# Nine modulation steps of layer two move from layer one's attention to the end of its routing

## The chip, the cores and the metric

The kernel runs on one core of a Trainium2 chip. The metric is the device time of one execution in microseconds. Each core has five engines that work in parallel, each with its own instruction queue: PE (matrix products; a weight load stands ahead of each product), DVE and ACT (element work), POOL (element work, and the DMAs with row numbers) and SP (here only DMAs). Transfers are carried out by 16 DMA engines that all queues share.

## The reference

Two layers of a transformer block over two streams of 256 tokens with 1024 channels: x (the image) and ctx (the context). Each layer starts from a modulation vector that depends on the conditioning alone. It then runs three kinds of attention, an output projection and a mixture of 16 experts, two of which each token uses.

```python
for l in range(DEPTH):
    mod = jnp.split(silu_c @ w_ada[l] + b_ada[l], 6, axis=-1)
    sh1, sc1, g1, sh2, sc2, g2 = [m[:, None, :] for m in mod]
    ...
    hx = rms_norm(x, norm1_g[l]) * (1 + sc1) + sh1
    hc = rms_norm(ctx, norm1_g[l]) * (1 + csc1) + csh1
    mix_x, mix_c = token_mixers(hx, hc, w_in[l], ...)
    x = x + g1 * (mix_x @ w_out[l])
    hx = rms_norm(x, norm2_g[l]) * (1 + sc2) + sh2
    x = x + g2 * moe_ffn(hx, w_router, router_bias, w_gate[l], w_up[l], w_down[l])
    ...
return rms_norm(x, final_g)
```

`moe_ffn` scores a token against the router, picks two experts and sums their gated outputs. In layer one ctx goes the same way as x; in layer two ctx serves only as keys and values.

## The kernel before, in words

**Tiles and stages.** Tokens stand in tiles of 128: tiles 0 and 1 are ctx, 2 and 3 are x. Layer one computes all four, layer two only 2 and 3. A layer has four stages: the projections of the modulated tokens (w_in), the attention, the output's projection (w_out) with the routing, and the experts. Weights are float32. Most are split into two float32r parts, `whi` by ACT and `wlo` by DVE, and a product is then three matmuls (lines 197 to 199, tiles `mm`).

**The modulation.** `ada_third` (line 426) computes 2048 columns of a layer's modulation, a third. Each of its first eight steps takes one unit of w_ada (128x2048, 1 MB) and makes four products 32x512 (tile `ada`, line 448). Then come DVE's addition of the bias (`modrow`, line 454) and four transposes with small copies. A third has 9, 10 or 9 steps. They are pulled by `fill(n)` from wherever the code calls it, in a fixed order: thirds 1 and 2 of layer one, then thirds 0, 1 and 2 of layer two. `FILL` says how many steps run among a layer's projections, in its attention and in its output's projection. Third 0 (sh1 and sc1) is needed at a layer's start; thirds 1 and 2 (g1, sh2, a2, g2) from the output's projection on.

**The attention.** `attention` runs a pipeline over items: 32 in layer one, 16 in layer two. Each tick carries steps of several items and ends with up to a few `fill` steps; the steps are spread evenly over the ticks from the first item's on. The last steps of an item come up to a few ticks after its values.

**Output's projection and routing.** `out_proj` goes over the two halves of w_out's columns (`cb`) and, in each, over the tiles. After each piece it calls `Route.logits`: a square sum on ACT, four transposes, a copy (`xT`) on ACT, and the router's four products (`rps`). After a tile's second half `Route.choose` normalizes the tile, writes it to DRAM (`h2row`, 0.5 MB, on SP's queue, line 1697) and picks the experts. After the last tile this is one long chain of small DVE steps, at whose end are the positions (`pps`) and the token numbers in each expert's list (`ips`, `idx`).

**Experts.** `experts` (layer one) gathers each expert's tokens from `h2row` by number with POOL's indirect DMA (`gather`, line 1005, tile `xg`), transposes them and runs gate, up and down. `LEAD` = 4 halves of weights are split ahead. `warm(20)` makes 20 products that nothing uses, ahead of the first gather. Layer two runs experts in pairs instead (`expert_pairs`).

**The weights' order.** `Ring` holds all raw weights in the order of use, which `queue` writes. It loads the next unit as soon as a slot is free for it, all on SP's queue, where the writes of `h2row` stand too. Slots of 1 MB: four "A" slots throughout, four more in layer one from the output's projection on ("B"), two more from the experts on ("C"). Each slot has a last layer, and a unit of layer two may only take slots that live in layer two, in layer one's stages that is the four A slots. A unit that finds no slot holds those behind it:

```python
slot = next((s for s in self.free if s[2] >= self.todo[0][0][1]), None)
if slot is None:
    break
```

A slot becomes free when the engine that reads it is done, and the load on SP waits for that. The order of instructions on each engine is set by the scheduler from the order of the code, except in stretches under `manual_schedule`, where the code's own order stands (the last tile's `choose` and the attention among them).

Of the kernel before, what the change touches and what calls it, by code (L numbers as in the profile page):

```python
# [20 lines left out]
PSUM = bass.MemoryType.PSUM  # L21
# [6 lines left out]
NONE = 1024  # L28
# [4 lines left out]
# columns of the packed constants  # L33
# [3 lines left out]
# slots for raw weights: throughout, from the output projection on, from the experts on  # L37
RAW = dict(A=4, B=(4, 3), C=(2, 5))
# halves of units as float32r parts: projections, their outputs' projections, experts
WSP = dict(proj=4, out=(4, 4), moe=5)  # L40
# banks of PSUM in the phases of a layer
# [3 lines left out]
PS_MOE = dict(gu=2, y=2, tp=2, hT=1)  # L45
PS_PAIR = dict(acc=4, gu=1, w=3)
# blocks of w_in's columns: kA, qA, kB vB kC vC, qB qC and vA
CBS = (4, 2, 1, 0, 3)
# steps of modulation (whole thirds) among a layer's projections, in its attention, in its output's projection
FILL = ((0, 28, 0), (9, 10, 0))  # L50
# tiles of projections that pass before one's transposes
LATE = 2
# heads of A and pairs of heads of B and C in the attention of two tiles of queries
ORDER = "aabababaabaabbbb"
# when the last steps of heads come: ticks after the values, and where in the tick (after the evacuation, after
# the maxima, at the end)
FINISH = dict(copy=(1, 1), squares=(2, 0), scale=(3, 2), turn=(4, 2), out=(1, 2))
# steps of a tick of attention, and the item of each, counted from the tick's
TICK = (("sums", 1), ("high", 5), ("transposes", 0), ("evacuate", 0), ("weights", 1), ("finish", 0), ("scores", 3),
        ("low", 5), ("maxima", 3), ("finish", 2), ("finish", 1), ("exps", 3), ("rest", -1), ("values", -1))  # L60
# halves of experts' weights that are ready ahead of their products
LEAD = 4
OVERFLOW = True
# products that keep the array's clock up before the experts
WARM = 20
# [6 lines left out]
def shape_constants():  # L72
    """Constants that depend on shapes alone, packed [128, C_END]."""
# [25 lines left out]
class Ring:  # L99
    """Weights in the order of their use, loaded ahead into whatever slots are free."""  # L100
# [11 lines left out]
    def open(self, pool, tag, n, last, queue=None):  # L112
        """n slots, for units of layers up to last"""
        self.free.extend((pool, f"{tag}{i}" if n > 1 else tag, last) for i in range(n))
        self.load(queue)
# [42 lines left out]
    def until(self, l, queue=None):  # L158
        """Only units that layers up to l use"""
        self.upto = l  # L160
        self.load(queue)
# [6 lines left out]
class Model:  # L168
# [18 lines left out]
    def transpose4(self, in_, n=4):  # L187
        """n 128 x 128 blocks of in_, transposed, in a bank"""
# [5 lines left out]
    def mm3(self, out, xh, xl, wh, wl, start, stop):  # L194
        """out += x^T w, each operand a sum of two float32r parts"""
# [11 lines left out]
    def rstd(self, pool, ss, n, width, tag):  # L207
        """(ss / n + eps) ** -0.5 over [128, width]"""
# [12 lines left out]
    def split(self, raw, lo, hi, engine=None):  # L221
        """A half of a unit of raw weights as an exact sum of two float32r parts."""
# [7 lines left out]
    def bcast(self, pool, tag, src, n, name, bufs=1, queue=None):  # L230
        """n elements in DRAM over all partitions"""
# [46 lines left out]
    def queue(self):  # L278
        """The weights in the order of their use."""
# [15 lines left out]
        def block(name, l, cb, n):  # L295
            for h in range(2):
# [3 lines left out]
                if name == "w_out" and h:  # L300
                    # rows of heads (kind, key head, query) to chunks of (kind, query)
# [6 lines left out]
        for l in range(2):  # L308
# [4 lines left out]
            for cb in range(2):  # L313
                block("w_out", l, cb, (0, 0))
                ada(sum(spread(FILL[l][2], 8)[4 * cb:4 * cb + 4]))
# [3 lines left out]
            for ps in range(self.npass[l]):  # L319
                for e in range(NEXP):  # L320
                    for n in ("w_gate", "w_up"):
                        ring.add((n, l, ps, e), a[n][l, e].rearrange("(p k) n -> p k n", k=NKC))
                    # an expert's second part comes after the next one's first
# [13 lines left out]
    def warm(self, n):  # L337
        """Products that nothing uses: the array's clock is to be up when the next ones come"""
# [5 lines left out]
    def paired(self, l):  # L344
        """Whether the experts of a layer go two at a time, with half a list each"""
        return l == 1 and self.npass[l] == 1
# [38 lines left out]
    def columns(self, tp):  # L385
        """From transposed rows of the modulation: stream, row of 512, chunk"""
        return tp.rearrange("p (c j q) -> p q j c", j=4, q=32)[:, 0:2]

    def ada_first(self, h):
        """Half the columns of the first layer's first shift and scale: those of even chunks of d land on partitions  # L390
        0 and 32 (c), 1 and 33 (c_ctx), those of odd chunks 64 partitions on"""
# [34 lines left out]
    def ada_third(self, l, third):  # L426
        """2048 columns of the modulation: the four 512s land on partitions 32j (c) and 32j+1 (c_ctx)."""
# [42 lines left out]
        elif third == 1:  # L470
            # what the shift adds to the router's logits, over all partitions
# [25 lines left out]
    # steps and the loads of units in a third of the modulation  # L497
    STEPS = (9, 10, 9)

    def fill(self, n):  # L500
        """n steps of the modulation among other work"""
# [3 lines left out]
    # rows of the modulation in DRAM: (third, half)  # L505
# [83 lines left out]
    def parameters(self, l):  # L589
        """The small parameters of a layer's attention"""  # L590
# [19 lines left out]
        def lam():  # L610
            """-(exp1 - exp2 + lam0)"""
# [6 lines left out]
    def tokens_in(self, l, tl):  # L618
        """Steps that bring tiles of a stream, normalized and modulated, to d on the partitions in Xh and Xl"""
# [22 lines left out]
        # the chunks of d in a bank  # L642
# [35 lines left out]
    def chunk(self, ps, tiles, kc, parts):  # L678
        """The products of tiles with a chunk of d of the first block of the projections"""
# [7 lines left out]
    def first_in(self):  # L687
        """The tokens of the first layer, half of d after the other, with the first block of its projections"""
# [51 lines left out]
    def next_in(self, l):  # L740
        """The tokens of a later layer, tile by tile, with the first block of its projections"""
        ps = {}
        with self.tc.tile_pool(name="cb", bufs=1, side="right", reuse_waits="tile") as cb, self.tc.manual_schedule():
# [44 lines left out]
            # the context's tokens have had their last use  # L788
# [3 lines left out]
    def parts(self, name, l, cb, fill=(0, 0)):  # L792
        """The halves of two units, split"""
# [9 lines left out]
    def units(self, name, l, cb, pairs, xh, xl, c0, parts):  # L803
        """The products of tiles of tokens with 512 columns of a weight, a group of tiles after another."""
# [1108 lines left out]
```

## Time and profile before

| | us |
| --- | --- |
| median of 3 runs | 902.95 (902.58 to 903.57) |
| span of the profiled execution | 900.9 |
| PE busy | 799.3 (89%) |
| DVE busy | 584.3 (65%) |
| ACT busy | 453.6 (50%) |
| POOL busy | 211.5 (23%) |

The span is that of one execution recorded by the profiler; the runs' times include a little around it, 2.05 us at the median. In a row of the time line the columns are start, duration, engine, line, operation, tile written and tiles read, shapes, count, and in brackets the idle time ahead of it with what ended it. Of layer one, the attention lies in about 140 to 264 us, the output's projection in 264 to 329, the last routing steps in 329 to 346 and the experts in 347 to 505.

### The profile page before, as it was taken

To read this page: it belongs to the slowest core of one execution; us is meant where nothing else is said; L and a number is where in the kernel's file an instruction comes from. 1 tells how busy PE (TensorE), PEld (TensorE's weight loads), DVE (VectorE), ACT (ScalarE), POOL (GpSimd) and SP (SyncE) were. 2 spreads that over 40 slices of the span, in tenths; PEclk is the share of its full clock that TensorE was granted. 3 is DMA by queue.
4 is the path that set the end of the run, shared out by engine and by line. 5 is a ranking of instruction groups with operands and counts; after the bars stand their busy time and mean duration, and the time that the engine had idled before them with its cause. 6 is when DMAs were issued, how large, how long until landed. Compare 5 with 4: busy or idle time off the path is not lost.

```text
span 900.9 us, 13085 instructions
## 1 busy us (share of the span) xinstructions
PE 799.3 (89%) x4807; PEld 584.2 (65%) x4807; DVE 584.3 (65%) x1192; ACT 453.6 (50%) x877; POOL 211.5 (23%) x244
## 2 busy tenths in 40 slices
PE   4899999989889977999999459999799869999992
PEld 1578877545546746999999348767566647666551
DVE  1577673897942698899999487677587563231224
ACT  2454432777652426888888456443387442121112
POOL 2010102473320133443432561000442000000100
PEclk9999999999998998999999769999999988999996
DMA  9952221666579537899993754287035965999921
GB/s 320 346 171 92 93 94 47 249 227 235 181 239 343 192 141 261 310 402 399 402 406 146 256 202 187 90 327 281 0 132 152 354 245 220 406 406 407 378 84 51
DMA packets 52537, 213.34 MB, mean 237 GB/s; under 512 B 9756, under 2 KB 9756, under 8 KB 34672
## 3 DMA queue, kind: packets, MB, share of 16 engines
q1 hardware_dynamic: 40832, 182.34, 54.4%
q0 software_dynamic: 6752, 19.08, 6.3%
q10 hardware_dynamic: 4880, 11.00, 3.2%
q8 instruction: 40, 0.66, 0.3%
q14 instruction: 33, 0.27, 0.1%
HBM read 204.99 MB, written 11.60 MB: 240 GB/s over the span
## 4 chain that ended last, share of the span: by engine, by line
PE 70%; DVE 14%; issue 4%; DMA 4%; ACT 4%; POOL 3%; ACTq 0%; SPq 0%; POOLq 0%; DVEq 0%
PE mm L199 8%; PE mm L197 8%; PE mm L198 8%; PE gu L1169 7%; PE tp L185 5%; PE gu L199 4%; PE w L1217 3%; PE gu L197 3%; PE gu L198 3%; PE ada L448 3%; DVE nm L1407 2%; PE w L1134 2%; PE sc L1393 2%; PE acc L1235 2%; PE y L197 2%
## 5 line engine op out<-in xcount | busy, mean ns | idle before, releaser
L227 DVE TENSOR_TENSOR wlo<-wraw,whi 128x1024 fp32r<-128x1024 f32 x136 | 186.5, 1391 | 51.9 <-ACT whi L226 51.1
L226 ACT CAST whi<-wraw 128x1024 fp32r<-128x1024 f32 x152 | 153.0, 1050 | 73.5 <-PE mm L199 39.1
L197 PE MATMUL mm<-whi,Xh 128*128 128x512 f32 x288 | 117.9, 409 | 5.1 <-ACT Xh L670 4.7
L198 PE MATMUL mm<-wlo,Xh 128*128 128x512 f32 x288 | 115.6, 401 | 0.4 <-DVE wlo L227 0.4
L199 PE MATMUL mm<-whi,Xl 128*128 128x512 f32 x288 | 115.3, 400 | 0.5 <-DVE Xl L674 0.5
L213 POOL TENSOR_TENSOR rstd<-ms,cst 128x1 f32<-128x1 f32 (+2 forms) x36 | 30.2, 838 | 315.0 <-DVE ms L211 306.1
L1420 ACT ACTIVATE e<-sc,nm 128x512 f32<-128x512 f32 (+1 forms) x96 | 58.3, 613 | 37.1 <-DVE nm L1413 19.2
L199 PE MATMUL gu<-whi,xl 128*128 128x256 f32 x256 | 73.9, 289 | 0.2 <-DVE xl L1030 0.2
L197 PE MATMUL gu<-whi,xh 128*128 128x256 f32 x256 | 73.7, 288 | 0.3 <-ACT xh L1029 0.3
L198 PE MATMUL gu<-wlo,xh 128*128 128x256 f32 x256 | 72.3, 282 | 0.0
L197 PEld LDWEIGHTS mm<-whi,Xh 128*128 128x128 f32 x288 | 54.9, 191 | 23.9 <-ACT Xh L670 6.2
L199 PEld LDWEIGHTS mm<-whi,Xl 128*128 128x128 f32 x288 | 54.9, 191 | 14.6 <-DVE Xl L674 1.5
L198 PEld LDWEIGHTS mm<-wlo,Xh 128*128 128x128 f32 x288 | 55.1, 191 | 13.1 <-DVE wlo L227 1.2
L1169 PE MATMUL gu<-wraw,xq 128*64 128x256 f32 x512 | 62.5, 388 | 0.0
L227 POOL TENSOR_TENSOR wlo<-wraw,whi 128x1024 fp32r<-128x1024 f32 x16 | 42.5, 2656 | 81.3 <-ACT whi L226 50.3
L199 PEld LDWEIGHTS gu<-whi,xl 128*128 128x128 f32 x256 | 48.9, 191 | 1.3 <-DVE xl L1030 0.6
L1169 PEld LDWEIGHTS gu<-wraw,xq 128*64 128x64 f32 x512 | 36.2, 138 | 20.8 <-issue 4.1
L197 PEld LDWEIGHTS gu<-whi,xh 128*128 128x128 f32 x256 | 49.1, 192 | 0.5 <-ACT xh L1029 0.5
L198 PEld LDWEIGHTS gu<-wlo,xh 128*128 128x128 f32 x256 | 49.0, 191 | 0.0
L185 PEld LDWEIGHTS tp<-ident,e 128*128 128x128 f32 x240 | 26.3, 143 | 34.7 <-issue 15.3
L1407 DVE TENSOR_REDUCE nm<-sc 128x1 f32<-128x512 f32 x64 | 41.6, 684 | 10.9 <-PE sc L1393 7.2
L1180 DVE TENSOR_TENSOR hid<-hid,gu 128x256 f32<-128x256 f32 (+1 forms) x9 | 3.8, 422 | 64.9 <-ACT hid L1179 64.9
(329 smaller groups left out, 1689.2 us busy)
## 6 DMA issues: line engine op xcount, KB each, us to landing
wraw<-in_w_ada SPq DMA_DIRECT2D x40, 1024.0 KB, 4.7
wraw<-in_w_gate SPq DMA_DIRECT2D x32, 1024.0 KB, 9.6
wraw<-in_w_up SPq DMA_DIRECT2D x32, 1024.0 KB, 9.9
wraw<-in_w_down SPq DMA_DIRECT2D x32, 1024.0 KB, 8.6
wraw<-in_w_in SPq DMA_DIRECT2D x16, 1024.0 KB, 6.9
wraw<-in_w_ada SPq DMA_DIRECT2D x16, 512.0 KB, 8.0
yrows<-y ACTq DMA_DIRECT2D x16, 512.0 KB, 7.4
wraw<-in_w_out SPq DMA_DIRECT2D x4, 1024.0 KB, 7.8
```

The source lines that it names most:

```text
L185: self.nc.tensor.transpose(out, in_, self.k["ident"][:n, :n])
L197: mm(out, lhsT=xh, rhs=wh, start=start, stop=False)
L198: mm(out, lhsT=xh, rhs=wl, start=False, stop=False)
L199: mm(out, lhsT=xl, rhs=wh, start=False, stop=stop)
L213: nc.gpsimd.tensor_tensor(r, ms, self.k["mhalf"][:, :width], OP.pow)
L226: nc.scalar.copy(h, raw[:, lo:hi])
L227: (engine or nc.vector).tensor_tensor(l, raw[:, lo:hi], h.bitcast(F32), OP.subtract)
L448: nc.tensor.matmul(ps[32 * j:32 * j + 32, :], lhsT=self.silu_c[:, kc, :], rhs=raw[:, 512 * j:512 * j + 512], start=kc == 0, stop=kc == NKC ...
L1169: nc.tensor.matmul(gu[PSLOTS * g:PSLOTS * g + PSLOTS, 256 * b:256 * b + 256], lhsT=xq[q][:, kc, c:c + PSLOTS], rhs=raw[:, kc * 256:kc * 25 ...
L1217: nc.tensor.matmul(y[hf][gs], lhsT=hT[:, c, 0:PSLOTS] if p == NP else hT[:, c, gs], rhs=raw[:, c * D + o * 512:c * D + o * 512 + 512], sta ...
L1407: V.reduce_max(self.nm[:, i:i + 1], self.ps[i], axis=AX.X)
L1420: nc.scalar.activation(self.e[i][:, :self.nkey], self.ps[i], AF.Exp, scale=0.125, bias=self.nm[:, i:i + 1], accum_out=self.z[i])
```

## The change

Layer one's attention keeps 19 of its 28 modulation steps, thirds 1 and 2 of its own layer. The nine of layer two's third 0 go to the end of layer one's routing. `TAIL` says where: two after the square sum of the last tile's second half, one after the copy of its transposes, one ahead of the logits' last products, one ahead of the positions, four ahead of the experts. `queue` puts their eight units behind both halves of w_out, ahead of the experts' weights. In both layers the attention's own steps are now spread over `len(items) - 5` ticks instead of `len(items) + 2`: 19 over 27 in layer one, 10 over 11 in layer two. `warm` makes 6 products instead of 20 and comes behind the gathers. The experts' stage has a bank of PSUM for the modulation.

```diff
-PS_MOE = dict(gu=2, y=2, tp=2, hT=1)
+PS_MOE = dict(gu=2, y=2, tp=2, hT=1, ada=1)
...
-FILL = ((0, 28, 0), (9, 10, 0))
+FILL = ((0, 19, 9), (9, 10, 0))
+SPARE = 5
+TAIL = (2, 1, 1, 1, 4)
...
-WARM = 20
+WARM = 6
...
 def queue(self):
             for cb in range(2):
                 block("w_out", l, cb, (0, 0))
-                ada(sum(spread(FILL[l][2], 8)[4 * cb:4 * cb + 4]))
+            ada(FILL[l][2])
...
 def attention(self, l):
-        fw = deque(spread(FILL[l][1], len(items) + 2))
+        fw = deque(spread(FILL[l][1], len(items) - SPARE))
...
 def out_proj(self, l, work, mods):
-        fw = spread(FILL[l][2], 8)
...
+                last = l == 0 and (t, cb) == (self.qtiles[-1], 1)
+                route.tail = iter(TAIL if last else ())
                 route.logits(t, cb)
-                self.fill(fw[cb * 4 + t])
...
 def experts(self, l, mo, lists):
-            self.warm(WARM)
             for n in range(3):
                 gather(n)
+            if l == 0:
+                self.fill(TAIL[-1])
+            self.warm(WARM)
...
 def logits(self, t, cb):
         nc.scalar.activation(junk, xs, AF.Square, accum_out=self.ss[:, i, cb:cb + 1])
+        m.fill(next(self.tail, 0))
...
         nc.scalar.copy(xT, m.transpose4(xs))
+        m.fill(next(self.tail, 0))
...
 def choose(self, x, i, r):
         lg = self.pps[:, 128 + i * 16:128 + i * 16 + 16]
+        m.fill(next(self.tail, 0))
...
+        m.fill(next(self.tail, 0))
         pps = self.positions(i)
```

**SP, from w_out's loads to the experts' first weights.** `wraw` is a slot of raw weights, `in_...` the weight it gets, `h2row` the normalized tiles in DRAM. Before:

```order
L149 DMA wraw<-in_w_gate 128x2048
L149 DMA wraw<-in_w_up 128x2048
L149 DMA wraw<-in_w_down 128x2048
L1697 DMA h2row<-h_3040 128x1024
L1697 DMA h2row<-h_3146 128x1024
L1697 DMA h2row<-h_3253 128x1024
L149 DMA wraw<-in_w_gate 128x2048
L149 DMA wraw<-in_w_up 128x2048
L1697 DMA h2row<-h_3363 128x1024
L149 DMA wraw<-in_w_down 128x2048
```

And after:

```order
L153 DMA wraw<-in_w_ada 128x2048 x4
L1706 DMA h2row<-h_2965 128x1024
L1706 DMA h2row<-h_3071 128x1024
L1706 DMA h2row<-h_3178 128x1024
L153 DMA wraw<-in_w_gate 128x2048
L153 DMA wraw<-in_w_ada 128x2048 x4
L153 DMA wraw<-in_w_gate 128x2048
L153 DMA wraw<-in_w_up 128x2048
L153 DMA wraw<-in_w_gate 128x2048
L153 DMA wraw<-in_w_up 128x2048
L1706 DMA h2row<-h_3313 128x1024
L153 DMA wraw<-in_w_down 128x2048
```

Between the third and the fourth write of `h2row` there are now nine loads instead of two, and of the experts' eight loads ahead of the first write none is left there.

**PE, from the last product of the output's projection on.** `x_107` is the last tile's second half, `rps` the router's products, `pps` positions, `ips` token numbers, `ada` the modulation. Before:

```order
L199 MATMUL mm<-whi,mixl 128x512
L185 MATMUL tp<-ident,x_107 128x128 x4
```

After:

```order
L203 MATMUL mm<-whi,mixl 128x512
L452 MATMUL ada<-wraw,silu_c 32x512 x8
L189 MATMUL tp<-ident,x_107 128x128 x3
L1759 LDWEIGHTS tri
L1759 MATMUL pps<-both,tri 128x16
L189 MATMUL tp<-ident,x_107 128x128
L452 MATMUL ada<-wraw,silu_c 32x512
L1770 LDWEIGHTS ohs
L1770 MATMUL ips<-val,ohs 128x16
L1770 LDWEIGHTS ohs
L1770 MATMUL ips<-val,ohs 128x16
L452 MATMUL ada<-wraw,silu_c 32x512 x3
```

Two steps (eight products) stand ahead of the last tile's transposes, one among them and the third tile's token numbers.

**PE, at the end of layer one's attention.** `e` and `onA` are weights and outputs of items, `poB` values, `modrow` the finished modulation. Before:

```order
L185 MATMUL tp<-ident,e 128x128 x8
L448 MATMUL ada<-wraw,silu_c 32x512 x4
L185 MATMUL tp<-ident,e 128x128 x8
L1567 MATMUL poB<-ptB,vBC 64x256 x8
L448 MATMUL ada<-wraw,silu_c 32x512 x4
L185 MATMUL tp<-ident,e 128x128 x8
L448 MATMUL ada<-wraw,silu_c 32x512 x4
L185 MATMUL tp<-ident,onA 128x128 x4
L1567 MATMUL poB<-ptB,vBC 64x256 x8
L448 MATMUL ada<-wraw,silu_c 32x512 x4
L185 MATMUL tp<-ident,modrow 128x128 x4
```

After:

```order
L189 MATMUL tp<-ident,e 128x128 x16
L1573 MATMUL poB<-ptB,vBC 64x256 x8
L189 MATMUL tp<-ident,e 128x128 x8
L189 MATMUL tp<-ident,onA 128x128 x4
L1573 MATMUL poB<-ptB,vBC 64x256 x8
L201 MATMUL mm<-whi,mixh 128x512 x2
```

Four steps' products and the transposes of `modrow` are gone from there, and the first products of the output's projection follow at once.

## Rows read from the trace of the kernel before

**Rows 1.** Busy time by stage; columns as in the first line
```profile
core 0: us, PE busy (x) PEld busy (x) DVE busy (x) ACT busy (x) POOL busy (x), PEclk, DMA share, GB/s
159.00:182.00 23.00, 22.40 (x165) 13.68 (x166) 19.79 (x55) 16.64 (x61) 11.60 (x20) 0.93 0.72 275
182.00:205.00 23.00, 18.93 (x126) 10.79 (x130) 21.52 (x59) 16.66 (x53) 16.04 (x28) 1.00 0.62 230
264.00:279.00 15.00, 10.00 (x30) 6.82 (x29) 5.57 (x9) 2.37 (x3) 0.90 (x2) 0.77 1.04 297
329.40:347.50 18.10, 8.88 (x57) 5.92 (x57) 16.81 (x79) 6.17 (x11) 6.97 (x8) 0.72 0.59 209
347.50:504.70 157.20, 155.02 (x1109) 144.59 (x1110) 142.00 (x140) 133.73 (x186) 62.00 (x30) 1.00 0.88 339
652.00:683.00 31.00, 29.67 (x207) 19.68 (x205) 26.74 (x65) 24.14 (x59) 13.54 (x23) 1.00 0.41 138
```

**Rows 2.** PE in time order, layer one's attention's end and first output tile
```profile
251.50 1.06 PE L448 MATMUL ada<-wraw,silu_c 128*32 128x512 f32 x8
252.84 0.66 PE L185 MATMUL tp<-ident,e 128*128 128x128 f32 x4 [0.27 <-ACT ptB L1557]
...
261.89 1.07 PE L448 MATMUL ada<-wraw,silu_c 128*32 128x512 f32 x8
263.77 0.66 PE L185 MATMUL tp<-ident,modrow 128*128 128x128 f32 x4 [0.81 <-DVE modrow L454]
...
271.62 0.49 PE L197 MATMUL mm<-whi,mixh 128*128 128x512 f32 x1 [3.55 <-ACT whi L226]
...
273.47 0.63 PE L199 MATMUL mm<-whi,mixl 128*128 128x512 f32 x1
273.89 0.63 PE L197 MATMUL mm<-whi,mixh 128*128 128x512 f32 x1
...
279.06 0.40 PE L199 MATMUL mm<-whi,mixl 128*128 128x512 f32 x1
```

**Rows 3.** Waits, 247 to 279: us in all, count, the longest
```profile
ACT whi L226 <- DMA wraw<-in_w_out: 8.2, 2, 6.2
```

**Rows 4.** DMA issues of SP: KB each, us to landing
```profile
wraw<-in_w_out SPq DMA_DIRECT2D x4, 256.0 KB, 18.6
...
wraw<-in_w_down SPq DMA_DIRECT2D x1, 1024.0 KB, 4.8
...
h2row<-h SPq DMA_DIRECT2D x1, 512.0 KB, 2.6
```

**Rows 5.** SP in time order, the last routing steps
```profile
329.16 0.33 SPq L149 DMA_DIRECT2D wraw<-in_w_gate  x1
...
337.37 0.33 SPq L1697 DMA_DIRECT2D h2row<-h  x1
```

**Rows 6.** PE in time order, the last routing steps
```profile
328.97 0.40 PE L199 MATMUL mm<-whi,mixl 128*128 128x512 f32 x1
332.22 0.63 PE L185 MATMUL tp<-ident,x 128*128 128x128 f32 x4 [2.85 <-DVE lt L1723]
...
346.18 1.06 PE L185 MATMUL tp<-ident,xg 128*128 128x128 f32 x8 [1.64 <-DMA xg<-h2row,idx]
```

**Rows 7.** POOL in time order, the first gather
```profile
341.81 1.17 POOL L1005 DMA_INDIRECT xg<-h2row,idx  x1 [5.92 <-DVE rows L1786]
```

**Rows 8.** Tile xg, all 16 gathers
```profile
DMA to landing us min/median/max: 4.2/9.1/10.4
```

**Rows 9.** Busy time, a stretch of layer two's experts that loads fill
```profile
764.00:830.00 66.00, 66.00 (x472) 40.89 (x471) 18.02 (x30) 14.59 (x32) 0.00 (x0) 1.00 1.00 403
```

**Rows 10.** PE in time order, layer two's attention's end
```profile
701.19 1.06 PE L448 MATMUL ada<-wraw,silu_c 128*32 128x512 f32 x8
...
704.88 0.63 PE L185 MATMUL tp<-ident,modrow 128*128 128x128 f32 x4 [2.63 <-DVE modrow L456]
706.30 0.63 PE L197 MATMUL mm<-whi,mixh 128*128 128x512 f32 x1
```

## Prediction

> **What bounds the kernel now.** I read the table by stage first [rows 1]. In layer one's experts (347.5 to 504.7 us) PE is busy for 155.0 of 157.2 us at full clock while the DMA engines are busy for 0.88: PE bounds that stage, and the whole stage starts when its first token rows arrive. In the first half of layer one's attention (159 to 182) PE is busy for 22.4 of 23 us; from 182 to 205 it is DVE that is nearly full (21.5 of 23). So a modulation step taken out of a PE-full tick saves its length, and one taken out of a DVE-full tick saves little.
>
> Then I read PE in order of time at the end of that attention [rows 2]. One modulation step is four products and four weight loads, 1.06 us. The last two stand at 261.89 and 263.77, the second behind a wait for DVE. The first tile of the output's projection then stops at 271.62 for a split of w_out, and the list of waits says that ACT stood 8.2 us for w_out's DMA [rows 3]. After the stop its products come 0.42 us apart (273.47, 273.89) at a duration of 0.63, against 0.40 from 279.06 on: the array's clock had fallen to half. In 264 to 279 the granted clock is 0.77 and the DMA share 1.04 [rows 1].
>
> Last I read the stretch between the last product of that projection (328.97) and the first transposes of gathered rows (346.18) [rows 6]. It is a chain of small DVE steps, PE busy for 8.9 of 18.1 us [rows 1]: the idle time that the change wants to fill. What ends it is the gather, issued at 341.81 once DVE has the row numbers [rows 7]. The last normalized tile is written to h2row at 337.37 [rows 5] and lands 2.6 us later [rows 4], at 340.0, so it is 1.8 us early and nobody waits for it.
>
> **Attention, layer one: a gain.** Nine steps leave it: eight with products and one with transposes. By ticks, three of them leave the first 27 ticks and the rest the end. Three at 1.06 us are 3.2 us at most; since part of these ticks is DVE-full I take 2.3. At the end, the step at 251.50 is followed by a wait of 0.27 us for ACT [rows 2], so it is mostly cover for ACT and worth nothing; those at 256 and 258 are worth about one together, since ACT and DVE follow one after the other there; the last (261.89) and the modrow transposes with their wait (263.77) go wholly, but the first split of w_out must still follow. I get the first product at 261.6 in place of 264.2: 2.6 us. Bounds for both together: 0 (DVE and ACT bind everywhere) and 9.5 (nine times 1.06). I take 4.9.
>
> **w_out: a gain.** Its four units follow the last modulation loads on SP and take slots that those free. The modulation now ends at tick 26, so all of w_out is there before the attention ends. The first tile's 24 products took from 264.2 to 278.6, 14.4 us; at 0.24 us each, with 0.8 for the first split, they take 6.6. That is 7.8 us; bounds 3.5 (the stop of 271.62 alone, if the clock falls all the same) and 8.6.
>
> **The last routing steps: a loss.** The products are covered: each step of 1.06 us stands where PE waits for DVE (3.3 us from 328.97 to 332.22, then longer) [rows 6]; one of them delays the router's products by about 0.9 us. DVE's additions (0.7 us and small copies) and POOL's (a memset and two small DMAs, 1.7 us) lie under POOL's 5.92 us of idle time ahead of the gather [rows 7]. Fewer warming products cost nothing if the modulation keeps the array busy.
>
> What is not covered are the loads. The ring gives its units out in order, and units of layer two may only take the four slots that live throughout. So the experts' loads, eight of which used to go out during the projection, now stand behind the modulation's last four, which wait for steps one to four of the tail. On SP there now stand, between the third and the fourth write of h2row, nine loads of 1 MB: w_gate, four of w_ada, and w_gate, w_up, w_gate, w_up. All are issued between the last product (329.2) and about 338.
>
> What a small DMA pays behind others on SP the trace shows: pieces of w_out of 256 KB, issued from 263.0 on behind other loads, landed after 18.6 us; a lone load of 1 MB takes 4.8 and a lone h2row 2.6 [rows 4]. At the rate of a saturated stretch, 403 GB/s [rows 9], 1.049 MB takes 2.60 us. The first of the nine, issued at 329.2 as its predecessor is now [rows 5], lands at 334.0, the ninth 8 x 2.60 later at 354.8, and h2row's 0.52 MB 1.3 us behind it at 356.1. The gather waits for all of h2row, so it is issued at 356.2 in place of 341.81: 14.4 us lost. Bounds: 0 (h2row is not held at all) and 16 (later steps delay the loads).
>
> The Trainium skill, page "DMA: Bandwidth & Descriptors", section "Queues, rings and completion order", says that every DMA engine takes a ring's descriptors in ring order and turns in rounds only between queues; by that a write on SP's own queue has no way round nine loads, and the 18.6 us agree. The same page (section "Where 436 GB/s comes from") gives a core about 358 GB/s from HBM; by that the nine would take 3 us longer and the sum below would be 8.5 instead of 5.5. The trace has 403, which decides.
>
> The gather itself then runs beside a full SP queue. Alone it took 4.4 us to the transposes (341.81 to 346.18); over all 16 it landed in 4.2 to 10.4 us, median 9.1 [rows 8]. I take 4.0 more, bounds 0 and 6.
>
> PE stands idle for some 15 us before it, so the array begins the experts at the lower clock, as at 271.62. That stretch of 7.4 us to 279.06 cost about 2.7 us beyond its waits; here I take 1.8, bounds 0 and 3.7 (half of 7.4).
>
> Nothing of this comes back in the experts: PE bounds them before, and their weights are loaded while PE waits, so they start with their slots full as before.
>
> **Layer two: a small gain.** Its ten steps stand in 11 ticks, not 18. Four more come into ticks where PE is busy for 29.7 of 31 us (652 to 683) [rows 1]: 3.2 us lost of 4.2. At the end the step at 701.19, the wait of 2.63 us for modrow at 704.88, and the slow products after it (0.63 at 706.30 [rows 10], against the 0.40 of 279.06) go, with three earlier steps worth 2.3: in all I get the first tile done 2.0 us sooner. Bounds: a loss of 1 and a gain of 4.5.
>
> **Sum.** -4.9 - 7.8 + 14.4 + 4.0 + 1.8 - 2.0 = +5.5 us. The profiled execution has a span of 900.9; the median of the runs, 902.95, is 2.05 above it, which I leave as it is. So the span becomes 906.4 and the time 908.5.
>
> **Rivals.** *h2row is not held (faster).* If its write is served beside the loads, by bytes and not by turn, it lands within some 5 us, and the gather goes at 342.7, when the delayed row numbers are there. It still takes up to 9 us under load, and w_gate itself lands only at about 347, so the experts begin 5.5 us late instead of 20.2: -14.7 + 5.5 = -9.2, or 893.8. For it: no row of before shows a single small write issued behind nine loads on SP, and the pieces of w_out that took 18.6 us were reads. Against it: the 18.6 us [rows 4]. The Trainium skill, same section as above, also says that completion is not in order of issue, since data descriptors carry no barrier; but that is about order within an engine's last writes, and no row here shows a write passing loads. The point where it decides: the sum is zero if h2row lands at 350.6, 5.5 us before my 356.1.
>
> *The tail costs less (even).* All as forecast, but the gather lands in 4.2 us under load and the cold array costs nothing: 5.5 - 4.0 - 1.8 = -0.3, or 902.7. For it: the first token rows are few bytes. Against it: the median of 9.1 [rows 8].
>
> *The attention does not get shorter (slower still).* If DVE and ACT bind its ticks everywhere, the 4.9 us are not there, and layer two's denser ticks cost 1: 908.5 + 4.9 + 3 = 916.4. For it: DVE at 21.5 of 23 us in 182 to 205. Against it: PE's 22.4 of 23 before [rows 1].
>
> **Chances.** Forecast 0.62, h2row not held 0.16, the even case 0.15, no shorter attention 0.07. A change of 0.2% (1.8 us) is about what a measurement of this kernel can tell from none. Faster by more: the first rival and a small part of the even case, 0.19. Within: most of the even case and the low end of the forecast, 0.14. Slower: 0.67. The range reaches from 898.5, where both attention gains and the cheap gather come together, to 916.0, the third rival; it leaves out the first rival.
>
> **What will show it.** Right: in the changed profile, PE waits for some 15 us ahead of the first transposes of gathered rows, with the DMA full; h2row's last write lands 15 us or more after issue; ACT no longer waits for w_out at the first tile; the clock in that tile stays at 1.00; w_ada's last loads are issued after the last product. Wrong: h2row landing in under 8 us, or a first tile that still stops, or experts that take less than 157 us.

## The result, and the profile after

The changed kernel took 918.82 us (median of 4 runs, 916.45 to 919.31) against 903.26 us before: a ratio of 1.0154, interval 1.0131 to 1.0178. It is slower, as forecast, but by 15.6 us where 5.5 were forecast; the time lies above the range. A second round gave 916.38 us and a ratio of 1.0131 (1.0110 to 1.0152), 12.7 us between the medians. The profiled execution has a span of 917.0 us, 16.1 above the one before.

What bounds the change is the stretch from the last product of layer one's output projection to the first gathered rows. PE in order of time, after, to be read against [rows 6]:

```profile
321.52 0.39 PE L203 MATMUL mm<-whi,mixl 128*128 128x512 f32 x1
321.84 1.92 PE L452 MATMUL ada<-wraw,silu_c 128*32 128x512 f32 x16
324.74 0.52 PE L189 MATMUL tp<-ident,x 128*128 128x128 f32 x3 [0.98 <-DVE lt L1732]
...
335.47 4.77 PE L452 MATMUL ada<-wraw,silu_c 128*32 128x512 f32 x22
341.05 0.65 PE L189 MATMUL tp<-ident,modrow 128*128 128x128 f32 x4 [0.81 <-DVE modrow L458]
341.54 0.82 PE L345 MATMUL tp<-mask,ones 128*128 128x256 bf16 x6
360.35 1.94 PE L189 MATMUL tp<-ident,xg 128*128 128x128 f32 x8 [17.99 <-DMA xg<-h2row,idx]
```

The modulation does fill the routing's idle time: the transposes of the last tile come 3.22 us after the last product (324.74 less 321.52), 3.25 before. But then PE waits 17.99 us for the gather, where it waited 1.64. The DMA issues of SP in that stretch, each an answer for a short window of its own, in the order of their issue at 329.04, 329.52, 329.99, 331.32, 331.81 and 333.49 (columns as in [rows 4], the last is us to landing):

```profile
wraw<-in_w_gate SPq DMA_DIRECT2D x1, 1024.0 KB, 11.9
wraw<-in_w_up SPq DMA_DIRECT2D x1, 1024.0 KB, 13.9
wraw<-in_w_gate SPq DMA_DIRECT2D x1, 1024.0 KB, 15.9
wraw<-in_w_up SPq DMA_DIRECT2D x1, 1024.0 KB, 18.3
h2row<-h SPq DMA_DIRECT2D x1, 512.0 KB, 19.1
wraw<-in_w_down SPq DMA_DIRECT2D x1, 1024.0 KB, 19.9
```

Issue plus time to landing gives 340.9, 343.4, 345.9, 349.6, 350.9 and 353.4: they land in the order in which they stand on the queue, with gaps of 2.5, 2.5, 3.7, 1.3 and 2.5 us, and the write of `h2row` takes its place among them. Before it landed 2.6 us after its issue [rows 4]. POOL's gather follows it:

```profile
341.05 0.52 POOL L435 MEMSET brow<- 128x512 f32 x1 [13.65 <-DVE modrow L458]
341.87 1.21 POOL L438 DMA_DIRECT2D brow<-in_b_ada  x2 [0.29 <-POOL brow L435]
343.08 0.97 POOL L1008 MEMSET xg<- 128x1024 f32 x1
351.74 1.13 POOL L1009 DMA_INDIRECT xg<-h2row,idx  x1 [7.70 <-DMA h2row<-h]
```

Before, the gather waited for DVE's `rows` [rows 7]. Here DVE writes `rows` at 334.25 and `idx`, the numbers that the gather reads, at 335.58, 16 us ahead of the gather. Counted from the last product, `rows` comes as before (12.7 us) and `idx` 2.3 us later (14.1 against 11.8).

The write is not all that stands in front of the gather. POOL first clears and reloads `brow`, the bias rows of the modulation, and for that it waits for `modrow`. So POOL was free for the gather only at 344.05, 22.5 us after the last product, against 12.8 us for the gather before. The write ends last, by 7.70 us, and hides a second delay of 9.7 us behind it.

Meanwhile the DMA engines are full (the same columns as [rows 1]; the second line is the experts' stage):

```profile
321.50:360.30 38.80, 16.26 (x105) 5.46 (x103) 18.53 (x83) 5.78 (x9) 9.15 (x11) 0.73 1.01 403
360.30:517.50 157.20, 156.16 (x1106) 146.25 (x1107) 141.70 (x139) 133.11 (x184) 59.91 (x29) 0.98 0.87 342
```

The gains came too, smaller. PE at the end of layer one's attention, after, against [rows 2]:

```profile
259.77 1.95 PE L1573 MATMUL poB<-ptB,vBC 128*64 128x256 f32 x16 [0.57 <-DVE mixl L1584]
263.13 0.73 PE L201 MATMUL mm<-whi,mixh 128*128 128x512 f32 x2 [1.42 <-ACT whi L230]
264.39 0.78 PE L202 MATMUL mm<-wlo,mixh 128*128 128x512 f32 x1 [0.53 <-DVE wlo L231]
...
267.53 0.55 PE L203 MATMUL mm<-whi,mixl 128*128 128x512 f32 x1
267.92 0.40 PE L201 MATMUL mm<-whi,mixh 128*128 128x512 f32 x1
```

The stop at the first tile is gone, and with it ACT's wait for w_out's DMA [rows 3]. What is left ahead of the first product is the split of w_out itself, 1.42 and 0.53 us, which the modulation's last step used to cover.

By stages, with two profiles of either kernel (the second pair from the experiments below; us, each from one row of PE or POOL to the next):

| stage | before, twice | changed, twice | difference of the means |
| --- | --- | --- | --- |
| start to layer one's first scores | 154.6, 155.3 | 155.8, 153.9 | -0.1 |
| attention, to the first product of the output's projection | 109.6, 110.1 | 107.3, 106.7 | -2.9 |
| that projection, to its last product | 64.8, 66.0 | 58.4, 56.8 | -7.8 |
| to the first gather | 12.8, 12.9 | 30.2, 29.5 | +17.0 |
| gather to the first transposes | 4.4, 4.4 | 8.6, 8.6 | +4.2 |
| to the last expert's last transposes | 155.1, 155.9 | 157.2, 156.5 | +1.3 |
| from there to the end | 399.6, 401.3 | 399.5, 399.6 | -0.9 |

They sum to +10.8. The first profile of either alone gives +16.1. The two sums differ because one program's executions do: the changed kernel's two profiles are 1.9 us apart in the first stage and 1.6 in the output's projection.

### The profile page after: what moved, and what is told of

It reads as the page before. It is cut to its first block, busy times and chain, and to the rows that moved or that the text cites. A ratio compares the mean times of both kernels' runs of the same rounds, so it can differ in the third digit from the quotient of the medians.

```text
span 917.0 us, 13044 instructions
## 1 busy us (share of the span) xinstructions
PE 802.4 (88%) x4793; PEld 587.1 (64%) x4793; DVE 583.1 (64%) x1192; ACT 454.1 (50%) x877; POOL 213.1 (23%) x244
## 5 line engine op out<-in xcount | busy, mean ns | idle before, releaser
L189 PEld LDWEIGHTS tp<-ident,e 128*128 128x128 f32 x240 | 26.7, 144 | 37.2 <-issue 19.1
L452 PE MATMUL ada<-wraw,silu_c 128*32 128x512 f32 x320 | 47.0, 637 | 1.7 <-DMA wraw<-in_w_ada 1.7
```

The source lines that it names most:

```text
L189: self.nc.tensor.transpose(out, in_, self.k["ident"][:n, :n])
L452: nc.tensor.matmul(ps[32 * j:32 * j + 32, :], lhsT=self.silu_c[:, kc, :], rhs=raw[:, 512 * j:512 * j + 512], start=kc == 0, stop=kc == NKC ...
```

## The experiments

Each is measured against the kernel before, run on the same chip in the same round.

**The write on another queue.**

```diff
-            nc.sync.dma_start(m.h2row[i * 128:i * 128 + 128, :], h2)
+            (nc.scalar if i == self.T - 1 else nc.sync).dma_start(m.h2row[i * 128:i * 128 + 128, :], h2)
```

> The changed kernel (918.8 us), but the last tile's write of h2row goes out on ACT's queue instead of SP's, behind nine loads. Theory (the write is held by its place on SP's queue): it lands within 7 us of its issue, since a lone one took 2.6 and it now shares the engines with one queue; the gather goes at about 339 instead of 351.7, 12.7 us earlier, and still takes some 8 us under load: 906 us, between 903 and 909. Rival (the 16 DMA engines are full, the queue does not matter): it lands as late as before, some 19 us after issue, and the time stays at 917 to 920.

Measured: 903.64 us, ratio 0.9993 (0.9979 to 1.0008), the kernel before 904.46. The write's issue and the gather in its trace:

```profile
h2row<-h ACTq DMA_DIRECT2D x1, 512.0 KB, 8.2
```

```profile
326.26 0.95 POOL L1008 MEMSET xg<- 128x1024 f32 x1
338.42 1.15 POOL L1009 DMA_INDIRECT xg<-h2row,idx  x1 [11.21 <-DMA h2row<-h]
```

The nine loads are the same and in the same order. The write lands after 8.2 us in place of 19.1, at 337.6; three loads issued ahead of it, at 327.94, 328.42 and 328.88, land after it, at 341.3, 343.8 and 347.6. So its place on SP's queue held it. The rival of full engines explains a smaller part, the 8.2 against 2.6 us alone. The gather goes 18.0 us after the last product in place of 30.2: 12.2 us of the theory's 12.7. The time stands at the low end of the range given.

Two things came with the edit that its line doesn't show. POOL now has the clearing of `xg` and the first three gathers ahead of the reload of `brow`; in the order of the changed kernel POOL would have been free only with `brow` done, so moving the write alone could have given no more than the 7.70 us by which the write ended last there. And SP's loads behind the nine wait 7.2 us for the write to land. How the 12.2 us divide between queue and POOL's order was not tested apart.

**Fewer loads ahead of the write.**

```diff
-            slot = next((s for s in self.free if s[2] >= self.todo[0][0][1]), None)
+            slot = next((s for s in self.free
+                         if s[2] >= (0 if self.todo[0][0][:3] == ("ada", 1, 0) else self.todo[0][0][1])), None)
```

> The changed kernel, but layer two's modulation units may also take the B slots, so that all eight are loaded during the output's projection; on SP five loads stand between the third and the fourth write of h2row instead of nine. Theory (each load ahead of the write costs its 2.6 us): the write lands 10.4 us earlier, 908.4 us, between 906 and 911. Rival (the delay belongs to the steps in the tail, whatever stands on SP): 916 to 920.

Measured: 907.32 us, ratio 1.0039 (1.0017 to 1.0060).

```profile
h2row<-h SPq DMA_DIRECT2D x1, 512.0 KB, 10.5
```

The gather goes 20.3 us after the last product instead of 30.2 and 29.5. Four loads fewer are worth 9.2 to 9.9 us, 2.3 to 2.5 each. Here POOL keeps the order of the changed kernel, with `brow` ahead of the gather, but is done with that at 338.80; the write lands at 341.3 and the gather goes at 342.11. Dose and effect agree; the rival would have left the wait.

**The early end alone.**

```diff
-        fw = deque(spread(FILL[l][1], len(items) + 2))
+        fw = deque(spread(FILL[l][1], len(items) - 5))
```

> The kernel before (903.3 us) with one part of the change: the attention's steps are spread over five fewer ticks than there are items, in both layers, and all 28 stay in layer one's attention. Theory (the stop at the first tile of the output's projection is w_out's late loads, and goes when the modulation ends earlier): the stop goes, 6.4 us as in the changed kernel, while 28 steps in 27 ticks cost the attention 0 to 3 us: 898 us, between 896 and 901. Rival (the stop went because nine steps and their loads went, not for the earlier end): it stays, and the time is 903 to 905.

Measured: 898.19 us, ratio 0.9936 (0.9917 to 0.9955), faster than both kernels. PE at the first tile of the output's projection:

```profile
265.88 0.72 PE L197 MATMUL mm<-whi,mixh 128*128 128x512 f32 x2 [1.42 <-ACT whi L226]
267.15 0.50 PE L198 MATMUL mm<-wlo,mixh 128*128 128x512 f32 x1 [0.54 <-DVE wlo L227]
267.48 0.40 PE L199 MATMUL mm<-whi,mixl 128*128 128x512 f32 x1
```

No stop, and all of the projection takes 56.8 us against 64.8 and 66.0: the gain of the changed kernel needs no step to leave the attention. The gather goes 12.7 us after the last product, as before. Its 28 steps in 27 ticks make the attention 110.95 us, 0.8 to 1.4 longer than before; a run below whose layer one is the same took 113.35, so this cost is known no better than that.

**Layer two's ticks.**

```diff
-        fw = deque(spread(FILL[l][1], len(items) - SPARE))
+        fw = deque(spread(FILL[l][1], len(items) + (2 if l else -SPARE)))
```

> The changed kernel, with layer two's ten steps spread over its 18 ticks as in the kernel before; layer one as changed. If the denser ticks of layer two are worth the 0.4 us that the two traces differ by after the first layer: 919.2 us, no difference that can be told. If they are worth the 2.0 us of the prediction: 920.8 us. If they cost something that another gain hides: below 918.

Measured: 914.19 us, ratio 1.0113 (1.0087 to 1.0139). That looked like a cost of the denser ticks, so the changed kernel was run again.

> The changed kernel once more, beside the next three on one chip. If the 4.6 us between it and the run with layer two's ticks undone were real, its ratio to the kernel before is again 1.015 and that run's 1.011; if they came from chips and clock, the ratio falls to 1.011 to 1.013: 914 to 916 us.

Measured: 916.38 us, ratio 1.0131 (1.0110 to 1.0152). The intervals overlap. The reverse edit, on the kernel that only ends early:

```diff
-        fw = deque(spread(FILL[l][1], len(items) - 5))
+        fw = deque(spread(FILL[l][1], len(items) + (2 if l else -5)))
```

> The kernel before with the fewer ticks in layer one alone; layer two as before, all 28 steps in layer one's attention. If layer two's denser ticks cost something (1.6 us in its attention, given back at its end), 897 us, 0.1 to 0.3% below the 898.2 of the run with both; if they gain the 2.0 us of the prediction: 900.2 us.

Measured: 900.13 us, ratio 0.9958 (0.9942 to 0.9974). That is what a gain of 2.0 us from the denser ticks gives, 0.2% above the 0.9936 of the run with both: the opposite sign, again with overlapping intervals. In the traces, layer two's attention takes 60.8 to 61.6 us to the last values with steps in 18 ticks (4 profiles) and 62.1 to 64.7 with steps in 11 (10 profiles), while from there to the first product it takes 5.95 in place of 3.36. What the denser ticks cost is given back at the end. From the first scores to the first product of the output's projection the four take 66.8 to 67.6 us, 67.0 in the mean, the ten 65.4 to 68.0, 66.6 in the mean: by the traces a gain of 0.4 us, which the spread could swallow.

**Both cures.** The edits of the first and the second experiment together.

> The changed kernel with both cures: the last write of h2row on ACT's queue and the B slots open to layer two's modulation. By the theory the gather goes once the row numbers are there or the write has landed some 8 us after its issue, no sooner than with ACT's queue alone; five loads in place of nine run beside it, so the write takes 5 to 8 us: 900 to 904 us. If loads beside the write cost nothing, 899; if the tail keeps a cost of its own, 904 or more.

Measured: 902.06 us, ratio 0.9986 (0.9971 to 1.0001). The gather goes 18.0 us after the last product, as with ACT's queue alone, and its rows take 9.4 us. The write takes 8.1 us to land, as with nine loads ahead of it. Only five stand ahead of it here, but SP issues four more from 328.12 to 330.14, around the write's own issue at 328.42, so as many loads are on their way beside it.

**A quiet DMA around the gather.** The B slots open as above, and:

```diff
+                if last:
+                    self.ring.until(-1)
...
-        m.fill(next(self.tail, 0))
+        k = next(self.tail, 0)
+        m.fill(k)
+        if k:
+            m.ring.load(n=k)
...
-        ring.until(l)
...
             if l == 0:
                 self.fill(TAIL[-1])
+            ring.until(l, nc.gpsimd)
```

> The changed kernel with the B slots open to layer two's modulation, so that its eight loads are done in the output's projection, and with the loads of the experts' weights held back: three (gate, up, gate) go out as soon as the first three steps have freed their slots, all others on POOL's queue behind the first three gathers. Theory (the whole loss is loads around the last write of h2row and the gather): the write lands in 2.6 to 4 us, the first gather goes 12.7 us after the last product of the output's projection and takes 4.4 us, as in the kernel before, while the attention stays short: 894 us, between 892 and 898. Rival (steps in the tail cost the routing chain itself, or the experts' weights come too late): 899 or more.

Measured: 913.63 us, ratio 1.0097 (1.0074 to 1.0121): 20 us above the theory's time. Its first signs failed too. The write, behind three loads, landed after 6.6 us, at 333.6, and the first gather went 17.3 us after the last product in place of 12.7 and took 6.3. In this run it is not the write that releases it, but POOL's own work:

```profile
332.01 0.52 POOL L435 MEMSET brow<- 128x512 f32 x1 [8.10 <-DVE modrow L458]
332.83 1.21 POOL L438 DMA_DIRECT2D brow<-in_b_ada  x2 [0.29 <-POOL brow L435]
334.03 0.97 POOL L1010 MEMSET xg<- 128x1024 f32 x1
335.29 1.20 POOL L1011 DMA_INDIRECT xg<-h2row,idx  x1 [0.29 <-POOL xg L1010]
```

So the steps in the tail do have a cost of their own, as the first half of the rival said: without `brow` the gather could have followed the write at about 334.4, an estimate from the 0.8 us between landing and gather in the runs above. The larger part of the loss is the rival's other half, late weights and gathers. It moved to the fourth, fifth and sixth gather, issued at 347.65, 352.28 and 361.35 on POOL's queue behind the seven loads that now stand there (DMA issues of POOL, each from a short window; the last column is us to landing):

```profile
xg<-h2row,idx POOLq DMA_INDIRECT x1, 34.2
xg<-h2row,idx POOLq DMA_INDIRECT x1, 32.7
xg<-h2row,idx POOLq DMA_INDIRECT x1, 25.8
```

```profile
PE tp L189 <- DMA xg<-h2row,idx: 20.4, 2, 12.2
```

The second fence is PE's wait in the list of waits, 341 to 390 us. It is the same trap on another queue: a small transfer that somebody waits for, put behind large ones that nobody needs yet. The experts' stage took 172.5 us.

**Steps spread to the end, nineteen of them.**

```diff
-        fw = deque(spread(FILL[l][1], len(items) - SPARE))
+        fw = deque(spread(FILL[l][1], len(items) - (SPARE if l else -2)))
```

> The changed kernel, with layer one's 19 attention steps spread over 34 ticks as before instead of 27; all else as changed. If the early end of the modulation took the stop from the output's first tile: the stop is back, 6 us, and the time is 920 to 923. If it was the smaller number of steps and loads: no stop, and the attention, with steps where ACT and DVE make PE wait, is no longer than the changed one's: 914 to 917.

Measured: 921.12 us, ratio 1.0177 (1.0146 to 1.0209), in the first theory's range, but not for its reason:

```profile
260.25 1.06 PE L452 MATMUL ada<-wraw,silu_c 128*32 128x512 f32 x8
263.95 0.63 PE L189 MATMUL tp<-ident,modrow 128*128 128x128 f32 x4 [2.63 <-DVE modrow L460]
265.50 0.76 PE L201 MATMUL mm<-whi,mixh 128*128 128x512 f32 x1 [0.92 <-DVE a L495]
```

There is no wait for w_out's loads. They stand behind 16 modulation loads instead of 24, the first is issued at 243.43 us where it was 252.63 before, and they are there in time. What is back is the modulation's own end, 3.8 us from the last values to the first product (7.1 against 3.4). So either edit removes the stop, the early end or the shorter list of loads; only the early end removes the wait for `modrow`.

**The array's clock at the start of the experts.** In the changed kernel, in two runs:

```diff
-WARM = 6
+WARM = 110
```

```diff
-WARM = 6
+WARM = 160
```

> The changed kernel with 110 products ahead of the first gathered rows instead of 6, so that PE works through most of the 18 us in which it waits. Theory (the array starts the experts at the lower clock and that costs what the two traces differ by in that stage, 157.2 against 155.1 us): the products of the first expert take 0.28 us from the start, 1.8 us gained: ratio 0.002 below the changed kernel's. Rival (the stage is longer for another reason, loads or splits): no gain.

> The changed kernel with 160 products ahead of the first gathered rows. In the run with 110 they took 0.11 us each and ended 7.3 us before the rows came, so the array was at the lower clock again when it began; 160 end about 1.8 us before. If the lower clock is what the first expert pays: its transposes take 1.06 us in place of 1.94, from there to the second expert's 7.7 us in place of 9.1 to 9.9, and the time falls by about 1.5 us. If not: 9 us or more between them, no gain.

Measured: 914.51 us, ratio 1.0121 (1.0103 to 1.0140), with 110, and 913.03 us, ratio 1.0104 (1.0070 to 1.0139), with 160. PE with 110, then with 160:

```profile
338.17 12.17 PE L345 MATMUL tp<-mask,ones 128*128 128x256 bf16 x110
357.62 1.94 PE L189 MATMUL tp<-ident,xg 128*128 128x128 f32 x8 [7.28 <-DMA xg<-h2row,idx]
```

```profile
336.50 17.63 PE L345 MATMUL tp<-mask,ones 128*128 128x256 bf16 x160
355.80 1.06 PE L189 MATMUL tp<-ident,xg 128*128 128x128 f32 x8 [1.68 <-DMA xg<-h2row,idx]
```

The 110 took 0.11 us each and ended 7.28 us early, and the transposes took 1.94 us as without them, so that run could not test the price. With 160 the pause was 1.68 us, the transposes took 1.06, and the experts' stage 154.96 us against 157.2 and 156.5 (156.4 with 110). The stretch of the first expert, in the changed kernel and then with 160 (columns as in [rows 1]):

```profile
360.30:370.20 9.90, 9.85 (x56) 9.38 (x57) 5.19 (x6) 5.41 (x7) 0.99 (x1) 0.67 0.91 360
355.00:365.00 10.00, 8.21 (x64) 7.55 (x64) 6.19 (x6) 6.85 (x9) 1.20 (x2) 1.00 1.01 401
```

In the changed kernel the granted clock stood at 0.50 of full speed, the lower level, from 348 to 360 us, with PE idle. From its transposes to the second expert's the first expert takes 9.9 and 9.1 us in the changed kernel at granted clocks of 0.67 and 0.74, and 7.7 with 160 at 1.00. So the idle array's lower clock costs the experts 1.4 to 2.2 us by the traces; the times alone, with intervals that overlap, don't tell it. The kernel before doesn't always escape it: its first expert takes 7.7 us at 1.00 in its first profile and 8.5 at 0.80 in its second, and the two kernels that only end early take 9.2 at 0.81, though their transposes still took 1.06.

**The kernel before again.**

> The kernel before once more, for a second profile of it: stages that no edit touches tell how far two executions differ. From the changed kernel's two profiles (head 1.9 us, first tile of the output's projection 1.6 us, experts 0.7 us apart): 901 to 905 us, with the experts of layer one 155 to 156.5 us.

Measured: one run of 907.75 us, span 905.9, above the range. Its experts took 155.9 us, its stop at the first tile 5.8 us in place of 3.55. It is the second column of the table above.

## Why the prediction was right in its sign and wrong in its size

**The held write: the right mechanism, and the first step that failed in its size.** 14.4 us were forecast for the gather's start, 17.0 came in the mean, beyond the bound of 16. It was the term that decided: in the trace the write's landing ends last, and the run with fewer loads moves it by 2.3 to 2.5 us a load. After the last product the gather was to go 27.2 us later (356.2 less 328.97); it went 30.2 and 29.5 us later. Three steps of that term were short in the first profile. The first load was to land 4.8 us after issue; it took 5.9, probably because the third write of `h2row`, issued 0.8 us ahead of it, was still under way. The eight others and the write were to follow in 22.1 us; they took 23.3. And from the write's landing (350.9) to the gather (351.74) 0.8 us pass where the sum had 0.1; with the write on ACT's queue it was 0.8 again (337.6 to 338.42). Together 3.0 us. The rival of a write that is not held falls.

The 18.6 us that spoke for the held write in the prediction were weak evidence: from 262.9 to 265.7 us, when those pieces of w_out were issued, POOL's queue took 73.4% of the time of the 16 engines and SP's 29.2%, so they paid for another queue too. That the mechanism held is shown by the runs, not by that row.

The Trainium skill, page "DMA: Bandwidth & Descriptors", section "Queues, rings and completion order", says that a DMA engine takes descriptors in ring order within a queue and takes turns between the queues that have work for it. The traces agree on both: 19.1 us in SP's queue behind the loads, 8.2 us on ACT's queue beside them.

**POOL's part of the modulation: put at nothing, and wrong.** It was to lie under POOL's idle time ahead of the gather. In fact it waits for `modrow`, and POOL was free for the gather 22.5 us after the last product, 9.7 us later than the gather went before. In the changed kernel the write hides this; in the run with the quiet DMA it shows. The rival's gain of 9.2 us rested on a gather at 342.7, 13.7 us after the last product, so with this order on POOL it could not have come even with a write that lands at once.

**The gather under load and the cold array: right.** 4.0 and 1.8 us were forecast; 4.2 and 1.3 came as a mean of two profiles, and the run with 160 products bears out the clock's part. The mean is under the 1.8 partly because the kernel before lost some of it too in its second profile. One stage of 156.5 us lies below the 157 that the prediction named as a sign against it. The even rival, with neither, falls.

**w_out: the mechanism right, the exact size luck.** 7.8 us forecast, 6.4 in the first pair of profiles, 9.2 in the second, 7.8 in the mean: the kernel before stopped for 3.55 us in one profile and for 5.81 in the other. One point was wrong all the same: the clock in the first tile was not sure to stay up. In the first profile its products took 0.63 us until 267.1, in the second 0.40 from 262.25 on, from the same program. That alone is 1.6 us.

**The attention: the second step that failed in its size.** 4.9 us forecast, 2.3 found in the first pair of profiles and 2.9 in the mean. Both estimates were too high, the one for the end above all. At the end 2.6 us were to go; 0.8 did, since ahead of the first product the split of w_out (1.42 and 0.53 us) is now in the open, which the last modulation step used to cover. "The first split of w_out must still follow" stood in the text, without its price. In the ticks 2.3 us were to go and some 2 did (first scores to last values 105.4 and 106.0 before, 103.9 and 103.4 after). The third rival, no shorter attention, named 916.4 us, near the measured time, but not for the right reason: the attention did get shorter.

**Layer two: too large, as far as is known.** 2.0 us forecast; from layer one's last expert to the end the kernels differ by 0.9 in the mean, up to layer two's first product of the output's projection the traces give 0.4, and the times of the two pairs of kernels that differ in its ticks alone point in opposite ways. The parts that the prediction named add to 2.8 us (1.06, 2.63 and 2.3 less 3.2) without the slow products, so its 2.0 was no sum of them.

**The sum.** By the means of two profiles the misses are the gather's start 2.6, the attention 2.0, layer two and what lies ahead of it 1.1 and the gather's load 0.2, less 0.5 for the cold array and 0.1 in the first stage: 5.3 us, which with the 5.5 forecast make the table's 10.8. So the forecast failed on the size of the held write, the attention and layer two, and all three misses made the time longer than forecast. The rest, up to the 16.1 us of the first pair of profiles, is what two executions differ by: that pair has 1.3 us more than the means in the first stage, which no edit touches, 1.4 in the output's projection, 0.8 in the experts, 0.8 behind them, 0.6 in the attention and 0.4 in the gather's start. The range took none of this in. Bounds on an edit's terms need the spread of one kernel's executions on top, here 1 to 2 us a stage, and 2.4 in the attention of the two kernels that only end early (110.95 and 113.35).

## What to carry to other kernels

A step moved into idle time brings its loads with it. Before moving it, list what then stands on each DMA queue ahead of the next transfer that somebody waits for; every MB cost 2.5 us here. It brings its work on the other engines too: here the reload of the bias rows stood ahead of the gather on POOL, and only the later write kept it from showing. On PE the steps delayed `idx` by 1.1 and 2.3 us in the two profiles, and nobody waited for that. Where two edits come in one change, time the cheap one alone: here the shorter spread of the steps by itself is 0.6% faster, and the move of the nine steps, together with it, 1.3 to 1.5% slower than before.

## What the runs showed of the hardware

- Loads and a write on one queue landed in the order of issue, about 2.5 us per MB; the same write on a second queue landed after 8.2 us, ahead of three loads issued before it on the first queue, against 2.6 alone.
- On POOL's queue the same was seen: gathers that land in 4.2 to 10.4 us [rows 8] took 25.8 to 34.2 behind seven loads.
- From the landing of a write to the start of the gather on POOL that needed it, 0.8 us passed in three runs (350.9 to 351.74, 337.6 to 338.42, 341.3 to 342.11).
- A pause of 7.28 us left the array at the lower clock (transposes 1.94 us), one of 1.68 us did not (1.06). The pause alone doesn't decide it: after 1.96 us in the second profile of the kernel before the transposes took 1.48 and the first expert had a granted clock of 0.80.
- Two executions of one program differ by 1 to 2 us in a single stage, in part by where the clock stands at the start of it (products of 0.63 or 0.40 us in the same first tile).
